# Writing a table to DRAM as one 3 MB transfer in the attention set-up, or as 16 transfers issued with the loads of the SSM stage

## Chip, cores and metric

One core of one Trainium2 chip. The metric is device microseconds of one execution. The kernel before takes 2279.62 us, the median of 3 runs (2279.33 to 2279.74).

## The reference

One layer of a hybrid decoder for a prompt of 2048 tokens and 8 sample tokens that share the weights. The input `x` is modulated, `h = x * (1 + scale) + shift`, and one product `h @ w_in` gives eight parts. `u_s` goes through a diagonal complex state-space model (SSM) of 64 groups, `q, k, v` through attention over a window of 128 keys, `z_s, z_a, g_s, g_a` are gates. Then follow a GLU product, two branch products, a gated merge, an output product and a LayerNorm.

The change concerns the relative bias of the attention, which depends on the distance of query and key alone:

```python
def rel_bias_from_dist(dist, rel_bias):
    b = rel_bias.astype(jnp.float32)[rel_bucket(jnp.clip(dist, 0, WINDOW))]
    return jnp.transpose(b, (2, 0, 1)).reshape(N_KV_HEADS, KV_GROUP, *dist.shape)
...
    s = s + rel_bias_from_dist(dist, rel_bias)
    s = jnp.where(mask[None, :, None, None], s, NEG_INF)
```

## The kernel before

**Products.** Every float32 matrix is split into a high and a low part (`split_w`, lines 49 to 60: a load into `wst`, of which there is one buffer, a cast on ACT, a subtraction on DVE), and a product is three matmuls (line 78). `products` (line 80) runs a list of jobs; a job is 128 columns of a weight against all 2056 tokens in five chunks (512, 256, 512, 264, 512 columns). A chunk is summed in one of three PSUM buffers `acc`, and an evacuation function then moves it through one of two SBUF buffers (`ev`) to DRAM. A buffer of `ev` is free again when its store has landed.

**Side work.** `products` calls `tick` three times a chunk, and each tick advances a generator of side work by one step. In phase 2 (`phase2`, line 847, 20 jobs, from 332 to about 900 us) the side work is the SSM: `ssm_pairs` (line 688) runs 32 pairs of groups through twelve steps (line 827), and a new pair starts every nine ticks. Step `load` (line 699) fetches the pair's constants `pk` (line 705) and its input `u` (line 707), each with two buffers. `b_mat` and `c_mat` are DVE work on `pk`; `t_mat` writes a small matrix `kt` to DRAM (`tD`, line 776) and reads it back skewed (`tt`, line 778); `x_in`, `scan` and `y_out` follow, and `y_out` multiplies `tt` with `u` (line 816). The first six jobs of phase 2 (`za_job`, line 540) store their chunks over SP's queue (line 550), the others over ACT's (lines 562 and 587).

**The bias table.** `attn_setup` (line 883) is the side work of the first job of phase 3. It loads a one-hot matrix `oh` and the bias `rb`, multiplies them (line 890), fills `fr`, 16 heads on 16 partitions by 384 numbers, with -1e30 (line 893), puts the scaled product in the middle (line 894), and writes each head's row 128 times to the DRAM tensor `biasD` (line 895: 3 MB, 2048 rows of 1536 bytes). Behind this it does the attention of the sample tokens (lines 897 to 976: caches `kc` and `vc`, scores, a softmax with an Exp on ACT at line 876, transposes on PE at lines 940 and 941). `attn_blocks` (line 978) then reads `biasD` with a row step of 383 (lines 1002 and 1003), so that the bias comes out shifted by one key per query.

**Order.** The order of each engine's instructions is made when the kernel is built: a list scheduler goes through the program with simulated times and gives each engine the instruction that stands first in the code of those that can go. Engines, and the queues on which SP and ACT issue transfers, then run in that order. Phase 2 pins nothing; lines 643 to 646 pin two copies to their place with `keep_in_program_order`. All transfers of SP and ACT are counted on eight semaphores in turn.

Of the kernel before, what the change touches and what calls it, by code (L numbers as in the profile page):

```python
# [9 lines left out]
F32 = mybir.dt.float32  # L10
# [29 lines left out]
class Trunk:  # L40
# [647 lines left out]
    def ssm_pairs(self, p, pp, ii):  # L688
        nc = self.nc
# [5 lines left out]
        for i in range(2):  # L695
            nc.sync.dma_start(tD[i][:, 0:112], zt)
            nc.sync.dma_start(tD[i][:, 256:368], zt)

        def load(s):
            pr = s["pr"]  # L700
            m, gl = divmod(2 * pr, 8)
            qd, gi = divmod(2 * pr, 16)
            s["m"], s["gl"] = m, gl
            s["pk"] = p.tile([128, 2, PK], F32, name="pk")
            nc.sync.dma_start(s["pk"], self.packD[qd][:, gi:gi + 2])
            s["u"] = p.tile([128, 2, 272], F32, name="u")
            nc.sync.dma_start(s["u"], self.uD[m][gl * 16:gl * 16 + 32].rearrange("c j n -> (c j) n")
                              .rearrange("(g q) n -> q g n", g=2))
# [115 lines left out]
        def gap(s):  # L824
            pass

        stages = [load, gap, b_mat, c_mat, t_mat, x_in, gap, scan, gap, gap, gap, y_out]
        return self.pipeline([{"pr": i} for i in range(32)], stages, ii)

# [50 lines left out]
        for h in range(nh):  # L880
            v.tensor_scalar(t1[:, h, kw], t1[:, h, kw], den[:, h:h + 1], None, op0=OP.mult)

    def attn_setup(self, p, pp):
        nc, I = self.nc, self.I
        oh = p.tile([32, 129], F32, name="oh")
        nc.sync.dma_start(oh, I["c_onehot"])
        rb = p.tile([32, 16], F32, name="rb")
        nc.sync.dma_start(rb, I["rel_bias"])
        pr = pp.tile([16, 129], F32, name="pt", bufs=2)
        nc.tensor.matmul(pr, rb, oh, start=True, stop=True)  # L890
        fr = p.tile([16, 384], F32, name="fr")

        nc.vector.memset(fr, NEG)
        nc.vector.tensor_scalar(fr[:, 127:256], pr, 8.0, None, op0=OP.mult)
        nc.sync.dma_start(self.biasD.rearrange("h (r l) -> h r l", l=384), fr[:, None, :].to_broadcast([16, 128, 384]))

        rr = p.tile([32, NS, 16], F32, name="rr")
        nc.vector.tensor_copy(rr, rb[:, None, :].to_broadcast([32, NS, 16]))
# [576 lines left out]
```

## Time and profile before

| | |
|---|---|
| median of 3 runs | 2279.62 us |
| profiled execution, its own time | 2282.66 us |
| its span, first to last instruction | 2280.9 us |
| mean granted TensorE clock | 0.992 |
| PE busy | 2228.4 us, 98% of the span |
| DVE, ACT, POOL busy | 1444.4, 787.7, 319.5 us |
| SP's transfer queue (q1), ACT's (q10) | 40.2%, 7.2% of 16 DMA engines |

All times in the rows are microseconds from the span's start. PE is TensorE's matmuls, DVE VectorE, ACT ScalarE, POOL GpSimd. SPq and ACTq rows are the issuing of transfers by SP and ACT. "L78" is line 78 of the kernel. `out<-in` names what an instruction writes and reads. In square brackets stands how long the engine was idle before it and what ended that.

### The profile page before, as it was taken

The page shows a single profiled execution, that of the slowest core. Times are in us where ns is not written, and L with a number is a line of the kernel's source. Part 1 is how long each engine was busy: PE and PEld are TensorE (multiplying, and loading weights), DVE is VectorE, ACT ScalarE, POOL GpSimd, SP SyncE. Part 2 cuts the span into 40 slices and gives each one's busy share as a digit, 9 for nine tenths or more (in the row PEclk, how much of TensorE's full clock was granted, in tenths as well). Part 3 has the DMA queues.
Part 4 walks back from the last instruction along what each step waited for, and adds up shares of the span by engine and source line. Part 5 has one row for each costly group of instructions (what it writes and reads, how often), then busy time and mean ns, then how long its engine had stood idle before and what let it go on. Part 6 is the DMA issues. An engine that isn't in the chain of part 4 may idle for free.

```text
span 2280.9 us, 35046 instructions
## 1 busy us (share of the span) xinstructions
PE 2228.4 (98%) x12571; PEld 1907.8 (84%) x12571; DVE 1444.4 (63%) x3572; ACT 787.7 (35%) x1700; POOL 319.5 (14%) x403
## 2 busy tenths in 40 slices
PE   7999999999999999899999999999979999999998
PEld 5888798888888888788888888888867888888886
DVE  4896219998888883168998888564454124124766
ACT  3411213332121111157777667573233123112100
POOL 1100001111111111000000000014541001222111
PEclk9999999999999999999999999999989999999999
DMA  9344523334443343743334343485347447667421
GB/s 298 103 141 143 181 96 111 115 114 119 121 117 114 114 123 110 128 126 112 114 113 138 108 119 107 113 192 180 111 143 231 124 127 241 184 186 229 158 96 72
DMA packets 387358, 317.98 MB, mean 139 GB/s; under 512 B 89318, under 2 KB 331006, under 8 KB 385599
## 3 DMA queue, kind: packets, MB, share of 16 engines
q1 hardware_dynamic: 349328, 260.02, 40.2%
q10 hardware_dynamic: 37856, 55.73, 7.2%
q8 instruction: 99, 1.62, 0.3%
q14 instruction: 75, 0.61, 0.1%
HBM read 195.24 MB, written 122.63 MB: 139 GB/s over the span
## 4 chain that ended last, share of the span: by engine, by line
PE 80%; DMA 8%; DVE 5%; SPq 3%; issue 2%; ACT 1%; POOL 1%; ACTq 0%; DVEq 0%; POOLq 0%
PE acc L78 58%; PE po L1413 8%; PE ps L1045 3%; PE po L1088 3%; PE pt L1072 2%; DMA z<-zsD 2%; PE acc L665 2%; DMA biasD<-fr 2%; SPq L178 1%; PE xp L784 1%; PE yp L817 1%; PE yp L816 1%; DMA tD<-kt 1%; DVE sg L1265 1%; DMA xst<-yD 1%
## 5 line engine op out<-in xcount | busy, mean ns | idle before, releaser
L78 PE MATMUL acc<-hh,whi 128*128 128x512 f32 (+2 forms) x2000 | 713.4, 357 | 0.1
L78 PE MATMUL acc<-hl,whi 128*128 128x512 f32 (+2 forms) x2000 | 704.7, 352 | 0.0
L78 PE MATMUL acc<-hh,wlo 128*128 128x512 f32 (+2 forms) x2000 | 702.9, 352 | 0.0
L78 PEld LDWEIGHTS acc<-hh,whi 128*128 128x128 f32 x2000 | 377.6, 189 | 49.2 <-issue 1.9
L78 PEld LDWEIGHTS acc<-hl,whi 128*128 128x128 f32 x2000 | 378.0, 189 | 48.8 <-issue 2.1
L78 PEld LDWEIGHTS acc<-hh,wlo 128*128 128x128 f32 x2000 | 377.6, 189 | 47.9 <-issue 0.8
L78 PE MATMUL acc<-xh,whi 128*128 128x512 f32 (+2 forms) x960 | 335.2, 349 | 16.3 <-ACT whi L58 16.3
L78 PE MATMUL acc<-xh,wlo 128*128 128x512 f32 (+2 forms) x960 | 333.8, 349 | 3.5 <-DVE wlo L59 3.5
L78 PE MATMUL acc<-xl,whi 128*128 128x512 f32 (+2 forms) x960 | 334.5, 349 | 0.0
L78 PEld LDWEIGHTS acc<-xh,whi 128*128 128x128 f32 x960 | 182.3, 190 | 40.8 <-ACT whi L58 17.6
L78 PEld LDWEIGHTS acc<-xh,wlo 128*128 128x128 f32 x960 | 181.9, 190 | 27.0 <-DVE wlo L59 4.1
L78 PEld LDWEIGHTS acc<-xl,whi 128*128 128x128 f32 x960 | 182.3, 190 | 22.9
L1059 ACT ACTIVATE t<-t,nm 128x256 f32<-128x256 f32 (+1 forms) x256 | 126.5, 496 | 48.0 <-DVE nm L1049 47.0
L59 DVE TENSOR_TENSOR wlo<-wst,whi 128x1024 fp32r<-128x1024 f32 x74 | 95.9, 1295 | 67.7 <-ACT whi L58 65.3
L1172 DVE TENSOR_TENSOR xl<-xst,xh 128x1024 fp32r<-128x1024 f32 (+2 forms) x84 | 97.1, 1176 | 57.9 <-ACT xh L1171 57.6
L58 ACT CAST whi<-wst 128x1024 fp32r<-128x1024 f32 x74 | 77.6, 1048 | 143.5 <-PE acc L78 121.9
L1171 ACT CAST xh<-xst 128x1024 fp32r<-128x1024 f32 (+2 forms) x84 | 86.2, 1046 | 93.3 <-PE po L1413 28.5
L1099 POOL TENSOR_TENSOR o<-o,z 128x512 f32<-128x512 f32 x32 | 43.4, 1355 | 520.5 <-DVE o L1093 474.3
L1049 DVE CUSTOM_DVE_ANT_0 t<-ps,bias,skb 128x256 f32<-128x256 f32 (+1 forms) x256 | 109.8, 471 | 5.9 <-issue 3.1
L1413 PE MATMUL po<-woh,xh 128*128 128x512 f32 (+1 forms) x272 | 103.4, 380 | 0.9 <-ACT woh L1335 0.9
L1413 PE MATMUL po<-wol,xh 128*128 128x512 f32 (+1 forms) x272 | 103.3, 380 | 0.8 <-DVE wol L1336 0.8
L1413 PE MATMUL po<-woh,xl 128*128 128x512 f32 (+1 forms) x272 | 103.3, 380 | 0.0
(359 smaller groups left out, 3318.6 us busy)
## 6 DMA issues: line engine op xcount, KB each, us to landing
wst<-in_w_in SPq DMA_DIRECT2D x50, 512.0 KB
uD<-u ACTq DMA_DIRECT2D x8, 1088.0 KB
u<-uD SPq DMA_DIRECT2D x32, 272.0 KB
yD<-y ACTq DMA_DIRECT2D x64, 132.0 KB
x<-in_x_prompt SPq DMA_DIRECT2D x16, 512.0 KB
wa<-in_w_ada SPq DMA_DIRECT2D x16, 512.0 KB
qf<-qD SPq DMA_DIRECT2D x32, 256.0 KB
z<-zaP SPq DMA_DIRECT2D x32, 256.0 KB
```

Source lines behind the costliest of these rows:

```text
L58: nc.scalar.copy(hi, st)
L59: nc.vector.tensor_tensor(lo, st, hi, op=OP.subtract)
L78: self.nc.tensor.matmul(ps[:, :n], w[:, k, :], x[:, k, :], start=(k == 0 and i == 0), stop=(k == KT - 1 and i == 2))
L665: nc.tensor.matmul(ps[:mt, :256], x[:, k, ts], w[:, k, :], start=(i == 0), stop=(i == 23))
L1045: nc.tensor.matmul(ps[:, a2, kw], s["q"][e][:, 2 * g + a2], kk[:, g, kw], start=(i == 0), stop=(i == 1))
L1049: v.tensor_tensor_reduce(t1[:, h, kw], ps[:, a2, kw], s["bias"][:, 4 * g + h, b0:b0 + kw.stop], -0.125, nsk[:, hs:hs + 1], OP.add, OP.min, ...
L1059: nc.scalar.activation(t1[:, h, kw], t1[:, h, kw], AF.Exp, bias=nm[:, h:h + 1], scale=-1.0, accum_out=den[:, h:h + 1])
L1072: nc.tensor.transpose(pt[:, a], s["t", g][:, a, h * 128:(h + 1) * 128], self.ident)
L1088: nc.tensor.matmul(pr, s["v"][h][:, g], x.rearrange("p a q -> p (a q)"), start=(h == hs[0] and i == 0), stop=(h == hs[-1] and i == 1))
L1171: nc.scalar.copy(xv(hi[:, k - 1:k + 1]), sv(st))
L1172: nc.vector.tensor_tensor(xv(lo[:, k - 1:k + 1]), sv(st), xv(hi[:, k - 1:k + 1]), op=OP.subtract)
L1413: nc.tensor.matmul(ps[:, :w], X[a][:, k, ts], Wo[h * w // 512][b][:, k, ws], start=(i == 0), stop=(i == 23))
```

## The change

The table is made at the start of phase 2, from `ssm_pairs`, and written there: step `load` of pairs 16 to 31 issues one transfer each, of one head's row 128 times (192 KB), ahead of the pair's own loads. `attn_setup` keeps its loads of `oh` and `rb`, which it needs for the sample tokens, and loses the rest.

```diff
@@ ssm_pairs
             nc.sync.dma_start(tD[i][:, 0:112], zt)
             nc.sync.dma_start(tD[i][:, 256:368], zt)
 
+        fr = self.bias_rows(p, pp)
+
         def load(s):
             pr = s["pr"]
+            if pr >= 16:
+
+                h = pr - 16
+                nc.sync.dma_start(self.biasD[h:h + 1].rearrange("h (r l) -> h r l", l=384),
+                                  fr[h:h + 1, None, :].to_broadcast([1, 128, 384]))
             m, gl = divmod(2 * pr, 8)
@@ attn_setup
+    def bias_in(self, p):
+        oh = p.tile([32, 129], F32, name="oh", bufs=1)
+        self.nc.sync.dma_start(oh, self.I["c_onehot"])
+        rb = p.tile([32, 16], F32, name="rb", bufs=1)
+        self.nc.sync.dma_start(rb, self.I["rel_bias"])
+        return oh, rb
+
+    def bias_rows(self, p, pp):
+
+        nc = self.nc
+        oh, rb = self.bias_in(p)
+        pr = pp.tile([16, 129], F32, name="tr", bufs=1)
+        nc.tensor.matmul(pr, rb, oh, start=True, stop=True)
+        fr = p.tile([16, 384], F32, name="fr", bufs=1)
+
+        nc.vector.memset(fr, NEG)
+        nc.vector.tensor_scalar(fr[:, 127:256], pr, 8.0, None, op0=OP.mult)
+        return fr
+
     def attn_setup(self, p, pp):
         nc, I = self.nc, self.I
-        oh = p.tile([32, 129], F32, name="oh")
-        nc.sync.dma_start(oh, I["c_onehot"])
-        rb = p.tile([32, 16], F32, name="rb")
-        nc.sync.dma_start(rb, I["rel_bias"])
-        pr = pp.tile([16, 129], F32, name="pt", bufs=2)
-        nc.tensor.matmul(pr, rb, oh, start=True, stop=True)
-        fr = p.tile([16, 384], F32, name="fr")
-
-        nc.vector.memset(fr, NEG)
-        nc.vector.tensor_scalar(fr[:, 127:256], pr, 8.0, None, op0=OP.mult)
-        nc.sync.dma_start(self.biasD.rearrange("h (r l) -> h r l", l=384), fr[:, None, :].to_broadcast([16, 128, 384]))
+        oh, rb = self.bias_in(p)
```

## Rows read from the trace of the kernel before

**Rows 1.** The page, part 1: busy time of each engine

```profile
PE 2228.4 (98%) x12571; PEld 1907.8 (84%) x12571; DVE 1444.4 (63%) x3572; ACT 787.7 (35%) x1700; POOL 319.5 (14%) x403
```

**Rows 2.** Waits of PE, whole span: us in total, times, longest

```profile
PE pt L940 <- DVE t1s L881: 5.8, 1, 5.8
```

**Rows 3.** Timeline of PE, 936 to 966: start, us, engine, what, count

```profile
943.34 0.39 PE L78 MATMUL acc<-hl,whi 128*128 128x512 f32 x1
949.51 0.45 PE L940 MATMUL pt<-ident,t1s 128*128 128x128 f32 x1 [5.79 <-DVE t1s L881]
...
950.39 0.63 PE L78 MATMUL acc<-hh,whi 128*128 128x512 f32 x1
...
954.97 0.40 PE L78 MATMUL acc<-hh,wlo 128*128 128x512 f32 x1
```

**Rows 4.** Stretch 950 to 960: us, busy of PE, PEld, DVE, ACT, POOL, granted clock, DMA share, GB/s

```profile
950.00:960.00 10.00, 10.00 (x57) 6.48 (x57) 2.14 (x4) 1.53 (x2) 0.00 (x0) 0.76 0.32 96
```

**Rows 5.** Timeline of ACT, 900 to 985

```profile
928.86 0.58 ACT L586 COPY zr<-acc 128x512 f32<-128x512 f32 x1 [10.67 <-DMA zsD<-zr]
...
946.76 1.28 ACT L876 ACT_TABLE_LOAD   x1 [0.47 <-DMA biasD<-fr]
948.06 0.40 ACT L876 ACTIVATE t1s<-t1s,nm 128x129 f32<-128x129 f32 x1
```

**Rows 6.** Timeline of DVE, 900 to 985

```profile
937.51 0.15 DVE L873 TENSOR_TENSOR es<-sk,mxs 128x1 f32<-128x1 f32 x1
```

**Rows 7.** Chain that ended last, 860 to 1060: start, us, what

```profile
909.93 36.83 DMA biasD<-fr
```

**Rows 8.** Timeline of SP's issues, 840 to 1010

```profile
904.01 0.55 SPq L886 DMA_DIRECT2D oh<-in_c_onehot  x1
...
909.93 0.68 SPq L895 DMA_DIRECT2D biasD<-fr  x1
918.99 33.92 SPq L55 DMA_DIRECT2D wst<-in_w_in  x2
```

**Rows 9.** SP's own waits, 900 to 1010: us in total, times, longest

```profile
SPq L55 <- DMA wst<-in_w_in: 28.5, 1, 28.5
...
SPq L1003 <- DMA zsD<-zr: 4.0, 2, 3.1
```

**Rows 10.** Line 1215, in the code of phase 4: durations, first and last start

```profile
L1215 SPq DMA_DIRECT2D bglu<-in_b_glu x1: 1268/1268/1268, 40.7 to 40.7; - x1
```

**Rows 11.** Timeline of SP's issues, 330 to 400

```profile
332.50 0.85 SPq L705 DMA_DIRECT2D pk<-packD  x1
...
336.12 0.47 SPq L705 DMA_DIRECT2D pk<-packD  x1
336.63 0.44 SPq L707 DMA_DIRECT2D u<-uD  x1
341.06 3.70 SPq L550 DMA_DIRECT2D zaP<-z  x2
...
349.04 0.38 SPq L778 DMA_DIRECT2D tt<-tD  x1
```

**Rows 12.** Timeline of PE, 351 to 354

```profile
352.51 0.61 PE L816 MATMUL yp<-u,tt 128*128 128x264 f32 x2
```

**Rows 13.** Transfer queues, 920 to 930: packets, MB, share of 16 engines

```profile
q1 hardware_dynamic: 615, 0.94, 87.8%
```

**Rows 14.** Transfer queues, 728 to 730, one store of 256 KB

```profile
q10 hardware_dynamic: 144, 0.26, 34.9%
```

**Rows 15.** Transfer queues, 330 to 332, one store of 128 KB

```profile
q10 hardware_dynamic: 144, 0.13, 19.4%
```

**Rows 16.** Stretch 700 to 750: us, busy by engine, clock, DMA share, GB/s

```profile
700.00:750.00 50.00, 50.00 (x275) 42.22 (x274) 42.46 (x90) 9.51 (x21) 10.54 (x14) 1.00 0.42 124
```

**Rows 17.** Timeline of SP's issues, 700 to 760

```profile
723.44 0.34 SPq L705 DMA_DIRECT2D pk<-packD  x1
```

**Rows 18.** Timeline of DVE, 703 to 745

```profile
725.93 0.49 DVE L716 TENSOR_TENSOR tmp<-pk 128x128 f32<-128x128 f32 x2
```

## The prediction

> **What bounds the kernel.** I read the page first: PE is busy for 98% of the span [rows 1], so whatever leaves PE idle is paid in full, and work on other engines costs only what makes PE wait. Next come PE's own waits. Of the places where it waits inside the phases that the change touches, one stands out: 5.8 us at line 940, for the softmax of the sample tokens [rows 2]. The timelines around it show why. PE had finished its last possible matmul at 943.34 and went on at 949.51 [rows 3]. Behind that wait the granted clock of 950 to 960 is 0.76 [rows 4]: for about half of the stretch PE ran at 1.2 GHz and not at 2.4, and matmuls of 512 columns took 0.63 us where they take 0.40 [rows 3]. DVE had everything ready for the Exp at 937.7 [rows 6], but ACT came to it only at 946.76 [rows 5], because ACT works in order and its copies ahead of it waited for an `ev` buffer, 10.67 us in the row shown, whose store had not landed [rows 5]. The stores were late because of the bias table. Its write lies on the chain for 36.83 us from 909.93 on [rows 7], and in 920 to 930 SP's queue holds 87.8% of the 16 DMA engines for 0.94 MB [rows 13]. SP's ring suffers as well: the weights asked for at 918.99 [rows 8] kept SP waiting for 28.5 us [rows 9].
>
> So the reader is to see two things: a stall of some 8 us that this write causes, and a write that is very slow for its 3 MB.
>
> **What the change removes.** If the write is gone from 909.93, ACT's stores land in time. The Exp then starts at 937.7 plus its table load of 1.28 us [rows 5, 6], and PE's transposes follow 949.51 - 948.06 = 1.45 us behind the Exp [rows 3, 5]: at 940.4, ahead of 943.34, so nothing is waited for. What is gained is 5.8 us, and the clock's share, 10 us x 0.24 = 2.4 us [rows 2, 4]: **-8.2 us**. Next behind it is nothing that PE waits for. The matmul of line 890, the memset and the scaling move to the start of phase 2 beside full engines, at 0.3 to 0.4 us each; I cost them at nothing either way. The loads of `oh` and `rb` are now made twice; two issues of half a microsecond on SP [rows 8] come ahead of the first `pk` load, and the cover is PE's matmuls of that stage, or one microsecond if it is gone.
>
> **What one new transfer costs.** No row has a transfer like it: 192 KB, read 128 times from one row of one partition. I bound it. Below: the old write, with 16 source partitions, moved 0.94 MB in 10 us [rows 13], so 196,608 bytes take 2.1 us if only the bytes count. Above: if each source partition gives no more than its share of that rate, one partition takes 16 times as long, 33 us. That the engines were not the limit is in the rows: 615 packets at 87.8% of 16 engines are 228 ns for 1536 bytes [rows 13], whereas a store from 128 partitions, each packet a row of its own partition, costs 11.17 engine-us for 128 packets of 2048 bytes [rows 14], 87 ns each. The source side set the pace. The nearest rows to one partition read by one engine at a time are the two stores: twice the bytes cost 11.17 - 6.21 = 4.96 engine-us more [rows 14, 15], that is 39 ns for 1024 bytes, 26 bytes per ns. At that pace 196,608 bytes take **7.4 us**, and I take this: a row of a partition given out at the best rate that any row shows for one, however many engines ask. Sixteen of them hold SP's rings for 119 us, where the single write needed 37.
>
> The Trainium skill, page "SBUF — State Buffer", section "Door 1: The DMA port swizzle", speaks against this change: transfers are limited by how many of 16 ports their partitions reach, it has 104 GB/s for partitions 0 to 15 and 27.6 GB/s for 0 to 3. This trace agrees on the first (94 GB/s in rows 13) and has nothing for the second; an estimate by that page is 7.1 us per transfer and 114 us for all, 5 us less in the sum below.
>
> **Where they stand in SP's order.** The code puts them in step `load` of pairs 16 to 31. But the trace shows that a transfer's place in the code doesn't hold it back: a load of phase 4 is issued at 40.7 [rows 10], and the loads of pair 1, nine ticks behind those of pair 0 in the code, went out at 336.12 and 336.63 right behind them and ahead of the first chunk's store at 341.06 [rows 11]. What held back later loads was a buffer that wasn't free. The new transfers need `fr` and nothing else. From the load of `oh` to the old write 5.9 us passed [rows 8]; with SP free for phase 2 at 332.5 [rows 11] the first transfer goes out at 338.4. SP issues one every 0.51 us (336.12 to 336.63), and in the 10.6 us up to the `tt` load of pair 0 at 349.04 [rows 11] 13 to 16 of them fit beside four of its own. So I expect all of them in a burst at the start of the stage, not in its second half.
>
> **What waits behind them.** SP's queue carries in this stage the stores of the first six jobs, `pk`, `u`, `tD`, `tt` and the weights. `tt` of pair 0 reaches PE 3.5 us after its issue (349.04 to 352.51) [rows 11, 12]; PE can't pass that matmul. With all 16 ahead, the rings are free at 338.4 + 119 = 457, PE goes on at 461 and has lost 108 us. With 13 ahead it goes on 22 us earlier and loses 86, and the last three then hold `z` stores for 22 us, of which PE covers some 14 with the chunks for which it has buffers (the same 14 that lie between 338.4 and 352.5): 94. I take 100. Stores on ACT's queue share the engines and wait too, as in [rows 5], but in these jobs they are few. A wait of this kind brings one slow stretch of the clock, 2.4 us [rows 4]. DVE's later work shifts with PE; its idle time, 7.5 us in 50 [rows 16], takes up the rest.
>
> **Sum.** The profiled execution takes 2282.66 us, 3 us above the median of the runs, of which 2280.9 are span; all terms are from it and I put them on the median: 2279.6 - 8.2 + 100 + 2.4 = **2374 us**. Its own range, with 86 to 115 us for the loss, is 2358 to 2390. Differences under 0.2% (4.6 us) can't be told from no change.
>
> **Rivals.**
> - *As written.* The transfers keep their places, one per pair in pairs 16 to 31, ahead of that pair's `pk` load. For it: the code. Against it: [rows 10, 11]. A `pk` load is used by DVE as soon as it is there (723.44 to 725.93, 2.5 us) [rows 17, 18], so 7.4 us in the ring ahead of it make DVE wait; it has 7.5 of 50 us idle [rows 16], 2.5 in the 17 us of a pair, and 4.9 x 16 = 78 us go to PE. 2279.6 - 8.2 + 78 = 2350.
> - *Cheap transfers in a burst.* Only the bytes count, 2.1 us each, 34 in all. The rings are free at 372, PE goes on at 376, 23 us late: 2279.6 - 8.2 + 23 + 2.4 = 2297. For it: the engines' sum is what [rows 13] shows. Against it: they all ask one partition.
> - *Hidden transfers, faster than before.* The transfers cost 2.1 us and stand one per pair; DVE's 2.5 idle us of each pair take them, and only the removed stall counts: 2271.4. It decides where a transfer takes less than 2.5 us and the code's places hold. Against it is what speaks against both of the above.
> - *The write doesn't cause the stall.* If other transfers make ACT late at 918 to 946, the 8.2 us stay: forecast 2382, hidden transfers 2279.6. [rows 13] leaves little room for others.
>
> **Chances.** Forecast 0.58, as written 0.12, cheap burst 0.12, faster 0.12, no change 0.03, much slower (towards 33 us per transfer) 0.03. The range leaves out the faster cases, no change and the far end: 2290 to 2400. Faster by over 0.2%: 0.12; within 0.2%: 0.03; slower: 0.85.
>
> **What would show it.** Right: sixteen issues of `biasD` at SP between 338 and 360; PE's waits led by line 816 or 817 for `tt`, or by `acc` for a `z` store, with about 100 us in all; the page's PE row low in the slices from 350 to 460; the row of line 940 gone and the clock of 950 to 960 (shifted) at 1.00. A wait of DVE at line 716 for `pk`, 16 times, would mean the code's places held. The forecast is wrong if SP issues the transfers elsewhere, or if in their stretch SP's queue moves much more than 27 GB/s.

## The result and the profile after

The changed kernel takes **2371.39 us** (median of 5 runs, 2370.73 to 2375.24) where the kernel before, run beside it, takes 2279.74 (2279.33 to 2281.26): ratio 1.041, interval 1.0397 to 1.0424. It is 91.7 us slower. Its profiled execution took 2371.21 us, of which 2369.3 are span.

The page of the changed kernel: span, busy time of each engine, then PE's busy share, its clock and the DMA share in 40 slices of 59.2 us, and SP's queue.

```profile
span 2369.3 us, 35075 instructions
...
PE 2231.8 (94%) x12571; PEld 1910.6 (81%) x12571; DVE 1441.6 (61%) x3572; ACT 788.3 (33%) x1700; POOL 321.3 (14%) x403
...
PE   7999991399999999999999999999979999999998
...
PEclk9999995699999999999999999999989999999999
DMA  9353638733343343333433533368337546667521
...
q1 hardware_dynamic: 349664, 260.04, 41.4%
```

The work is the same as in [rows 1]: as many matmuls, as much busy time within 4 us. But in two slices, 355 to 474 us, PE stands nearly still while the DMA engines are at their fullest since the first slice. PE's idle time, span less busy, rose from 52.5 us [rows 1] to 137.5, by 85.0; its busy time rose by 3.4. Together that is the whole difference of the spans, 88.4 us.

PE's waits in the changed kernel, whole span (us in total, times, longest):

```profile
PE yp L823 <- DMA tt<-tD: 62.6, 2, 60.5
PE tr L752 <- DVE bt L725: 22.5, 1, 22.5
...
PE tr L752 <- DVE kt L779: 9.1, 1, 9.1
```

The wait at the softmax [rows 2] is gone, and these three came, 94.2 us together. Line 823 is line 816 of the kernel before, the matmul that needs `tt`; `bt` is what DVE makes of `pk`. Their places on PE's timeline (the idle time before each in brackets):

```profile
366.17 0.66 PE L752 MATMUL tr<-ident,bt 128*128 128x128 f32 x2 [9.09 <-DVE kt L779]
...
432.31 1.25 PE L823 MATMUL yp<-u,tt 128*128 128x264 f32 x2 [60.51 <-DMA tt<-tD]
...
465.10 0.66 PE L752 MATMUL tr<-ident,bt 128*128 128x128 f32 x2 [22.50 <-DVE bt L725]
```

In [rows 12] PE passed the matmul of `tt` at 352.51; here it does so at 432.31. Why `tt` came so late stands on the timeline of SP's issues (start, time that SP spent on them, line, what, count):

```profile
336.40 0.47 SPq L712 DMA_DIRECT2D pk<-packD  x1
336.91 0.43 SPq L714 DMA_DIRECT2D u<-uD  x1
340.61 0.32 SPq L550 DMA_DIRECT2D zaP<-z  x1
343.83 1.21 SPq L706 DMA_DIRECT2D biasD<-fr  x2
345.14 4.30 SPq L550 DMA_DIRECT2D zaP<-z  x1
349.84 18.13 SPq L706 DMA_DIRECT2D biasD<-fr  x3
368.07 5.62 SPq L550 DMA_DIRECT2D zaP<-z  x1
373.74 15.11 SPq L706 DMA_DIRECT2D biasD<-fr  x3
388.95 7.24 SPq L550 DMA_DIRECT2D zaP<-z  x1
396.23 5.17 SPq L706 DMA_DIRECT2D biasD<-fr  x2
401.50 11.88 SPq L783 DMA_DIRECT2D tD<-kt  x2
413.43 2.71 SPq L706 DMA_DIRECT2D biasD<-fr  x2
420.14 3.35 SPq L785 DMA_DIRECT2D tt<-tD  x1
423.53 19.64 SPq L706 DMA_DIRECT2D biasD<-fr  x4
443.27 7.25 SPq L712 DMA_DIRECT2D pk<-packD  x1
```

All 16 transfers of the table go out at the start of the stage, between 343.83 and 443, not in its second half. Twelve of them stand ahead of `tt`, which is issued at 420.14 and not at 349.04 [rows 11], and four behind it, ahead of `pk` of the third pair; that `pk` is the 22.5 us at line 752. The third wait, 9.1 us at 366.17, is a `z` store: ACT could not write its next `z` before a store behind the first two transfers of the table, issued at 345.14, had landed, and DVE's `z` and `kt` stood behind ACT (waits in 350 to 370):

```profile
ACT z L546 <- DMA zaP<-z: 16.7, 1, 16.7
DVE z L547 <- ACT z L546: 15.8, 1, 15.8
```

The second column of SP's timeline was not foreseen: 18.13 us for three issues. Over all 16 (shortest, median and longest in ns, first and last start):

```profile
L706 SPq DMA_DIRECT2D biasD<-fr x16: 568/3975/7305, 343.8 to 435.9; - x16
```

SP could not pass its transfers on any faster than the queue took them.

The queues in 345 to 445, the GB/s in 40 slices of 2.5 us, and packets, MB and share of 16 engines:

```profile
GB/s 30 28 26 28 26 66 42 27 29 26 26 66 43 76 53 27 28 28 25 28 28 28 81 27 26 27 28 30 63 28 27 27 28 27 81 28 24 28 28 28
...
q1 hardware_dynamic: 2986, 3.53, 84.9%
```

Wherever only the table moves, the rate is 24 to 30 GB/s, with the engines 84.9% busy. The packets of the table, the only ones of 1536 bytes, begin at 345.05, and the last of them starts at 460.62: 115.6 us for all 16, 7.2 us each.

Stretches of the changed kernel (us, busy of PE, PEld, DVE, ACT, POOL, granted clock, DMA share, GB/s):

```profile
376.00:400.00 24.00, 0.00 (x0) 0.00 (x0) 0.00 (x0) 0.86 (x2) 0.00 (x0) 0.51 0.85 36
400.00:420.00 20.00, 0.00 (x0) 0.00 (x0) 0.00 (x0) 0.00 (x0) 0.00 (x0) 0.50 0.81 39
...
1040.00:1060.00 20.00, 20.00 (x126) 15.53 (x125) 2.77 (x7) 3.83 (x12) 0.00 (x0) 1.00 0.33 89
```

From 376 to 420 all engines stand still but for two instructions of ACT (0.86 us). The transpose that ended the old stall, line 940 of the kernel before, now starts at 1042.9; in 1040 to 1060, which answers to [rows 4], PE is busy throughout at a clock of 1.00: the old stall is really gone.

### The profile page after: what moved, and what is told of

It reads as the page before. It is cut to its first block, busy times and chain, and to the rows that moved or that the text cites. A ratio compares the mean times of both kernels' runs of the same rounds, so it can differ in the third digit from the quotient of the medians.

```text
span 2369.3 us, 35075 instructions
## 1 busy us (share of the span) xinstructions
PE 2231.8 (94%) x12571; PEld 1910.6 (81%) x12571; DVE 1441.6 (61%) x3572; ACT 788.3 (33%) x1700; POOL 321.3 (14%) x403
## 4 chain that ended last, share of the span: by engine, by line
PE 82%; DMA 6%; SPq 4%; DVE 4%; issue 2%; POOL 1%; ACT 1%; DVEq 0%; ACTq 0%; POOLq 0%
PE acc L78 60%; PE po L1429 7%; PE ps L1061 3%; PE po L1104 2%; DMA z<-zsD 2%; PE pt L1088 2%; PE acc L665 2%; SPq L706 2%; PE xp L791 1%; SPq L178 1%; PE yp L823 1%; PE yp L824 1%; DMA pk<-packD 1%; DMA tD<-kt 1%; DMA zaP<-z 1%
## 5 line engine op out<-in xcount | busy, mean ns | idle before, releaser
L1188 DVE TENSOR_TENSOR xl<-xst,xh 128x1024 fp32r<-128x1024 f32 (+2 forms) x84 | 97.7, 1181 | 52.5 <-ACT xh L1187 51.9
```

Source lines behind the costliest of these rows:

```text
L1188: nc.vector.tensor_tensor(xv(lo[:, k - 1:k + 1]), sv(st), xv(hi[:, k - 1:k + 1]), op=OP.subtract)
```

## The experiments

The theory: a transfer's price is set by the source partitions that it reads, the 16 go out in a burst because nothing holds them to their place, and what PE lost is `tt`, `z` stores and `pk` behind them. The rivals: the bytes or the number of issues cost it; the place does, whatever is put there; the code's place held. The medians of the kernel before beside these runs were 2279.08, 2279.24 and 2278.11.

**Same bytes, same issues, same place, other source partitions.** The row of each head is made on 8 partitions; transfer h writes one 1536-byte row from each of the 128.

```diff
-        nc.tensor.matmul(pr, rb, oh, start=True, stop=True)
-        fr = p.tile([16, 384], F32, name="fr", bufs=1)
+        nc.vector.tensor_copy(r8, rb[:, :, None].to_broadcast([32, 16, 8]))
+        nc.tensor.matmul(pr, r8.rearrange("b h s -> b (h s)"), oh, start=True, stop=True)
+        fr = p.tile([128, 384], F32, name="fr", bufs=1)
...
-                nc.sync.dma_start(self.biasD[h:h + 1].rearrange("h (r l) -> h r l", l=384),
-                                  fr[h:h + 1, None, :].to_broadcast([1, 128, 384]))
+                nc.sync.dma_start(self.biasD.rearrange("h (s r l) -> (h s) r l", s=8, l=384)[:, h:h + 1],
+                                  fr[:, None, :].to_broadcast([128, 1, 384]))
```

> Edit: the changed kernel with the same 16 transfers of the same 196,608 bytes at the same place in the code, but fr is held on 128 partitions (8 copies of each head's row) and each transfer reads one row from every partition. Number of issues, bytes and place stay; only the source partitions of a transfer differ. Theory (a transfer is paced by its single source partition, 7.2 us; the lost time is tt behind about 115 us of such transfers): each transfer takes 0.6 to 1.5 us (192 KB at the rate of a store from 128 partitions, 11.17 engine-us for 128 packets of 2048 bytes, is 1.05 us), all 16 done within 25 us, PE's waits at tt fall from 62.6 to under 15 us, time 2275 to 2290 us. Rival 1 (the bytes or the number of issues cost it, whatever the source): 2360 to 2375 us. Rival 2 (DRAM rows are the limit, not the source): transfers stay at about 7 us, 2360 to 2375 us.

Measured: 2275.42 us, ratio 0.9986 (0.9977 to 0.9995). The burst is still there, 16 issues from 344.6 to 355.1, all ahead of `tt`, which follows at 357.54. Its busy times, its issues of the table, and its queue in 346 to 356:

```profile
PE 2224.9 (98%) x12571; PEld 1906.0 (84%) x12571; DVE 1442.7 (63%) x3573; ACT 788.2 (35%) x1700; POOL 325.3 (14%) x403
```

```profile
L706 SPq DMA_DIRECT2D biasD<-fr x16: 320/450/617, 344.6 to 355.1; - x16
```

```profile
q1 hardware_dynamic: 2604, 3.24, 93.3%
```

3.24 MB pass in 10 us where the changed kernel needed 100 for 3.53. An issue takes SP 0.45 us in the median, against 3.98 in the changed kernel. So neither the bytes, nor the 16 issues, nor the place of the burst cost much: 96 of the 2371 us hang on the source partitions. (The 1.05 us of the expectation are twice what its own rows give, 0.52 over 16 engines; measured are 0.6.) One thing more changes with this edit: the rows of one transfer land 24 KB apart in DRAM and not in one run of 192 KB, and no run changes that alone. The run with the heads in another order, below, speaks for the source: there each transfer still writes its run of 192 KB. In spans, 2369.3 less 2273.2, that is 89.2 us of PE's idle time and 6.9 of busy time at a slower clock.

**The move alone: one transfer of 16 heads at the start of the stage.**

```diff
         fr = self.bias_rows(p, pp)
+        nc.sync.dma_start(self.biasD.rearrange("h (r l) -> h r l", l=384), fr[:, None, :].to_broadcast([16, 128, 384]))
...
-            if pr >= 16:
...
```

> Edit: the changed kernel, but one transfer of all 16 heads (16 source partitions, the form that the kernel before had in its later stage) right behind the rows of fr, at the start of the SSM stage. Theory (rate goes with the source partitions): this transfer takes 33 to 38 us in place of 115, tt of pair 0 lands some 80 us earlier than in the changed kernel, PE's waits there are 15 to 35 us in place of 94, time 2287 to 2310 us. Rival (the place is what costs, whatever the transfer's length): 2350 to 2375.

Measured: 2298.21 us, ratio 1.0081 (1.0066 to 1.0096). `tt` is issued at 382.33. PE waits 18.3 us for `z`, whose stores stood behind the table, and 3.5 for `tt`. The queue in 350 to 380:

```profile
q1 hardware_dynamic: 2100, 3.09, 88.5%
```

That is 103 GB/s from 16 partitions. The move costs 19 us net, not 92.

**The split alone: 16 transfers in the old place.**

```diff
-        nc.sync.dma_start(self.biasD.rearrange("h (r l) -> h r l", l=384), fr[:, None, :].to_broadcast([16, 128, 384]))
+        for h in range(16):
+            nc.sync.dma_start(self.biasD[h:h + 1].rearrange("h (r l) -> h r l", l=384),
+                              fr[h:h + 1, None, :].to_broadcast([1, 128, 384]))
```

> Edit: the kernel before with its one transfer split by head into 16, in its old place behind the SSM stage; nothing is moved. This is the other half of the change alone (e_one_early is the move without the split: 2298.21 us). Theory (split by head, each transfer reads one partition and takes 7.2 us wherever it stands): 115 us in place of 37 for the whole write, from 910 to about 1026, the wait at the softmax of the sample tokens grows from 5.8 us and new waits for stores and for the reads of the table come behind it; 78 us longer for the rings, of which PE covers a part, so 2310 to 2365 us. Rival (the price of 7.2 us belongs to the place at the start of the stage, where other transfers compete): the 16 take 40 to 60 us in all, 2275 to 2295.

Measured: 2345.22 us, ratio 1.0299 (1.0282 to 1.0316). The packets run from 914.5 to 1019.3, 105 us, and SP is held for nearly all of that at its issues; PE waits in the stage behind:

```profile
911.21 97.29 SPq L896 DMA_DIRECT2D biasD<-fr  x16
```

```profile
PE acc L78 <- ACT zr L586: 49.1, 2, 41.6
PE pt L942 <- DVE t1s L881: 11.6, 1, 11.6
PE po L964 <- DVE so L959: 3.0, 1, 3.0
```

The price does not belong to the place. The split costs 67 us where the old write stood, and there the old stall grows from 5.8 to 11.6 us.

**The places held.** Each transfer is pinned to its place in the program's order.

```diff
-                nc.sync.dma_start(self.biasD[h:h + 1].rearrange("h (r l) -> h r l", l=384),
-                                  fr[h:h + 1, None, :].to_broadcast([1, 128, 384]))
+                self.tc.keep_in_program_order(
+                    nc.sync.dma_start(self.biasD[h:h + 1].rearrange("h (r l) -> h r l", l=384),
+                                      fr[h:h + 1, None, :].to_broadcast([1, 128, 384])))
```

> Edit: the changed kernel with each of the 16 transfers pinned to its place in the order of the program, so that they go out one by one over the second half of the SSM stage, as the code says. Price of a transfer as before, 7.2 us from one partition. Theory (burst ahead of tt is where the time went, and the price is per transfer): PE's waits at 366 to 465 us are gone, no transfer of the table before 600 us; each transfer still takes about 7.2 us of SP's rings and a load asked for behind it lands so much later. What that costs was put at 78 us (4.9 us in each of 16 pairs, 2350 us) if pk is used as soon as it is there; if SP's rings have room for it, between 0 and 30 us (2272 to 2305). Rival (the transfers cost the same wherever they stand, since each holds SP's rings): 2360 to 2375.

Measured: 2337.55 us, ratio 1.0254 (1.024 to 1.0268). The 16 issues are spread over the second half, the first at 563.7 (none was expected before 600) and the last at 900.9, and PE's stall at 366 to 465 is gone. Its busy times, the issues, PE's waits in 550 to 940, and that stretch (its granted clock is the third number from the end):

```profile
PE 2245.2 (96%) x12571; PEld 1918.8 (82%) x12571; DVE 1442.1 (62%) x3572; ACT 788.5 (34%) x1700; POOL 321.5 (14%) x403
```

```profile
L707 SPq DMA_DIRECT2D biasD<-fr x16: 492/510/4789, 563.7 to 900.9; - x16
```

```profile
PE yp L824 <- DMA tt<-tD: 24.8, 6, 5.3
PE yp L825 <- DVE S L816: 16.1, 5, 8.2
```

```profile
550.00:940.00 390.00, 349.14 (x1770) 289.41 (x1769) 274.28 (x574) 63.39 (x129) 50.30 (x106) 0.94 0.54 107
```

So the burst accounts for about 34 us of the loss, and a spread-out write at this price still costs 64 against the next experiment: 4.0 us in each of 16 pairs. The expectation left a gap between 30 and 78 us, and the result fell into it, nearer to its upper end. Two thirds of it are waits; the rest is a slower clock, 0.94 in this stretch where the next experiment has 1.00. Against the next experiment, which differs in the source alone, PE is idle for 40.6 us more (87.1 against 46.5) and busy for 21.0 us more (2245.2 against 2224.2).

**The places held and the cheap source**: the pin and the 128 source partitions together.

```diff
+                self.tc.keep_in_program_order(
+                    nc.sync.dma_start(self.biasD.rearrange("h (s r l) -> (h s) r l", s=8, l=384)[:, h:h + 1],
+                                      fr[:, None, :].to_broadcast([128, 1, 384])))
```

> Edit: the transfers pinned to their places in the second half of the SSM stage as in e_pin, and each read from 128 partitions as in e_16_128. This is the change as its code says, with a cheap transfer. Theory (price and burst are two separate causes; at about 1 us a transfer is hidden beside pairs that have 2.5 us to spare): the wait at the softmax is gone and nothing takes its place, 2269 to 2273 us, as in e_128_old (2270.24). Rival (16 more issues in SP's queue among the loads of the pairs cost by themselves): 2275 to 2285.

Measured: 2273.09 us, ratio 0.9975 (0.9965 to 0.9984). At 0.6 us a transfer (3.24 MB in 10 us, above) it is hidden, and only the old stall goes. The time is at the upper end of what was expected, 2.9 us above the last experiment below; the intervals of the two don't tell them apart.

**Four transfers of four neighbouring heads.**

```diff
-            if pr >= 16:
+            if pr >= 16 and pr % 4 == 0:
...
-                nc.sync.dma_start(self.biasD[h:h + 1].rearrange("h (r l) -> h r l", l=384),
-                                  fr[h:h + 1, None, :].to_broadcast([1, 128, 384]))
+                nc.sync.dma_start(self.biasD[h:h + 4].rearrange("h (r l) -> h r l", l=384),
+                                  fr[h:h + 4, None, :].to_broadcast([4, 128, 384]))
```

> Edit: the changed kernel with four transfers of four heads each (4 neighbouring source partitions, 786,432 bytes) in place of 16 of one head; the bytes, the place and the burst stay. Two readings of the slow source are told apart. Reading A (a group of four neighbouring partitions shares one way out of about 27 GB/s): each transfer takes 28 to 30 us, 112 to 118 us in all, time 2360 to 2376, as in the changed kernel. Reading B (each partition gives about 27 GB/s by itself): each takes 7 to 8 us, about 30 us in all, time 2280 to 2300.

Measured: 2388.18 us, ratio 1.048 (1.0466 to 1.0494). The queue in 350 to 406 (56 us):

```profile
q1 hardware_dynamic: 1008, 1.47, 22.6%
```

Again some 25 GB/s, with the packets of all four running from 346.0 to 468.3, 122 us: as reading A has it. The share matters here: 22.6% is between three and four of 16 engines' worth of time. Four partitions by some four engines give what one partition gave to some fourteen (84.9%), so neither the engines' time nor the single partition set the rate; it fits a limit that the four neighbours share. By itself this run leaves a rival: with only some four engines at work, each packet takes 0.20 us (22.6% of 16 engines, 1008 packets in 56 us), and if that were what an engine needs for a packet of a repeated row, the rate would be the same. Two runs speak against it: in the last experiment below each row is repeated 16 times and a packet takes 0.065 us (101.1% of 16 engines for 1742 packets in 7 us), and the next run changes the order of the heads alone. The Trainium skill, page "SBUF — State Buffer", section "Door 1: The DMA port swizzle", gives 27.6 GB/s for partitions 0 to 3 and 104 for 0 to 15; the runs agree with 25 and 103. The time came out 12 us above what was expected: here one `z` store stands at SP behind the second transfer and another behind the fourth, and PE waits 54.5 and 50.7 us behind ACT, which waits for them.

**The heads in another order**: 0, 4, 8, 12, 1, 5, ...

```diff
-                h = pr - 16
+                h = pr % 4 * 4 + pr // 4 % 4
```

> Edit: the changed kernel with the heads in the order 0, 4, 8, 12, 1, 5, ... so that neighbouring transfers read from different groups of four partitions; everything else stays. In the changed kernel the one transfer that followed another of a different group took 5.5 us and the others 7.0 to 7.5. Theory (groups of four are the limit, and a ring works its transfers off in order, so two transfers overlap only at their ends): 5 to 6 us each, 80 to 100 us in all, PE's waits there 60 to 78 us, time 2338 to 2358. Rival A (several transfers in flight at once, each on its own group): about 30 to 45 us in all, 2285 to 2305. Rival B (no overlap): 2365 to 2375.

Measured: 2339.97 us, ratio 1.0267 (1.0252 to 1.0283). The packets run from 345.6 to 429.7, 84 us, 5.3 each. The order of the transfers alone is worth 31 us. The queue in 362 to 366, in which only the table moves:

```profile
q1 hardware_dynamic: 166, 0.22, 81.5%
```

That is 55 GB/s, twice the rate of the changed kernel, at about the same share of the engines. So transfers from two groups of four pass side by side, where neighbours of one group do not, and this is what shows the group. They do so for a part of the time only: four side by side throughout would take about 29 us in all, not 84. That they overlap just at their ends, because the queue works them off in turn, is the theory's reading.

**Another queue**: the transfers issued by POOL.

```diff
-                nc.sync.dma_start(self.biasD[h:h + 1].rearrange("h (r l) -> h r l", l=384),
+                nc.gpsimd.dma_start(self.biasD[h:h + 1].rearrange("h (r l) -> h r l", l=384),
```

> Edit: the changed kernel with the 16 transfers issued from POOL's queue and not from SP's; source, bytes and place in the code stay. Theory (what PE lost was tt, z stores and loads behind the transfers in SP's own queue, and SP held up at issuing them): the transfers still take 7 us each or more, 115 us or more in all, but tt of pair 0 is landed within 10 us of its issue and PE's waits at 366 to 465 are under 40 us, time 2285 to 2325. Rival (the 16 DMA engines themselves are held, so the queue makes no difference): PE's waits there 80 us or more, 2355 to 2380.

Measured: 2354.18 us, ratio 1.033 (1.0316 to 1.0344). This is against the theory's number and near the rival's, 0.8 us under its range: PE waits 81.3 us in one piece for `tt`. Its queues in 350 to 400, and SP's issues:

```profile
q0 software_dynamic: 502, 1.54, 91.3%
q1 hardware_dynamic: 374, 0.46, 3.8%
```

```profile
340.75 17.73 SPq L550 DMA_DIRECT2D zaP<-z  x4
358.60 23.47 SPq L783 DMA_DIRECT2D tD<-kt  x2
440.06 0.38 SPq L785 DMA_DIRECT2D tt<-tD  x1
```

POOL's queue (q0) holds 91.3% of the engines for 31 GB/s, and SP's gets 0.46 MB through in 50 us. `tt` itself passes quickly now, but the `tD` stores that it reads, asked for from 358.60 on, land only at 426 and 440. So in this run the slow transfers held up SP's queue from another one, and the move to it saved 17 of the 92 us.

**The old place and form, but the source on 128 partitions** (one transfer of all heads in the kernel before).

```diff
-        nc.sync.dma_start(self.biasD.rearrange("h (r l) -> h r l", l=384), fr[:, None, :].to_broadcast([16, 128, 384]))
+        nc.sync.dma_start(self.biasD.rearrange("h (s r l) -> (h s) r l", s=8, l=384),
+                          fr[:, None, :].to_broadcast([128, 16, 384]))
```

> Edit: the kernel before with its one transfer in its old place, but fr on 128 partitions (8 copies of each head's row), so that the write reads 128 partitions and not 16. Theory (the write is slow by its source partitions, and its 37 us make ACT's stores late and PE wait at the softmax of the sample tokens): the write takes 8 to 12 us, that wait of 5.8 us and the slow clock behind it are gone, time 2271 to 2274 us, 0.2 to 0.4% under the kernel before. Rival (the stall has another cause): 2278 to 2281.

Measured: 2270.24 us, ratio 0.9964 (0.9952 to 0.9977), the lowest median of all and a little under the expected 2271. The write's packets run from 914.1 to 923.2, 9.1 us. The queues in 915 to 922, and two stretches:

```profile
q1 hardware_dynamic: 1742, 2.68, 101.1%
```

```profile
940.00:950.00 10.00, 10.00 (x54) 7.59 (x56) 1.70 (x3) 1.53 (x2) 0.00 (x0) 1.00 0.31 94
950.00:960.00 10.00, 10.00 (x75) 7.92 (x68) 1.07 (x4) 2.30 (x10) 0.00 (x0) 1.00 0.32 84
```

2.68 MB in 7 us is 383 GB/s where the old write had 94 [rows 13]. PE waits for nothing from 900 to 1000, and the clock of 950 to 960 is 1.00, not 0.76 [rows 4]. What the change wanted, the stall away, is had without moving anything: 8.8 us by the medians.

## Why the prediction was right

It gave 2374 us and 2290 to 2400; the time is 2371.39. Step by step:

- *The stall that is removed, -8.2.* Right. The kernel with the fast write in its old place gained 8.8 us, with an interval from 5.2 to 10.9, and lost both the wait and the slow stretch behind it.
- *One transfer, 7.4 us between 2.1 and 33.* Right: 7.2. The pace of 26 bytes per ns that was read from two stores [rows 14, 15] stands in the profile after as 24 to 30 GB/s. But the reason given, a row of one partition given out at its best rate, was too narrow: four partitions together give no more. That the pace fitted is in part luck, since those two stores don't tell the pace of an engine from that of its source. The text's sum for all 16 was 119 us; measured were 115.6. The estimate by the Trainium skill, page "SBUF — State Buffer", section "Door 1: The DMA port swizzle", 7.1 us and 114 in all, came nearer.
- *Not held to their place.* Right: all 16 went out at the start, and pinning them moved them to the second half. Begun at 343.8 and not at 338.4, because `fr` was ready 5.4 us later than put.
- *13 to 16 of them ahead of `tt`.* A near miss, and by luck. It was 12, but the way of counting failed: SP began at 343.8, and at 0.51 us per issue only ten would have fitted in up to 349.04. The time that SP has at run time doesn't set the order; the order is made when the kernel is built. The changed kernel and the one with the heads in another order issue in the same sequence, 12 ahead of `tt`, though SP was held there for different times; with the source on 128 partitions all 16 stand ahead. Nor did the working have the held issues, 3.98 us in the median and up to 7.3.
- *100 us lost.* 94.2 us by the three waits. PE passed the matmul of `tt` 79.8 us later than in [rows 12], where 86 were put for 13 transfers ahead; 69.6 of these were idle (9.1 for the `z` store and 60.5), and the rest PE filled with other work. What came behind cost more than put: 22.5 us for `pk` of the third pair, where the step had 8 for `z` stores and did not name `pk`. The two errors offset each other.
- *The clock, +2.4.* PE's busy time rose by 3.4 us although the old slow stretch went (2.4), so the new ones cost about 5.8: it was mis-sized, since there are three waits and not one.
- *The sum.* By the profiled executions 2371.21 - 2282.66 = 88.6, by the medians 91.7; the prediction's terms add up to 94.2. Its own range, 2358 to 2390, is a little wider than what 86 and 115 us give, 2360 to 2389.

Of the rivals, *as written* was priced at 78 us for 16 places held; the pinned kernel shows 64. The wait for `pk` which that rival named is there, 27.6 us in 5 waits of DVE, but DVE waits longer for `tD` (35.8 us in 9), and what PE waits for is `tt` and the scan behind it. *Cheap transfers in a burst* is the kernel with 128 source partitions: 2275.42 against 2297 put, because a transfer costs about 0.6 us there, not 2.1. *Hidden transfers* is the pinned kernel with that source: 2273.09 against 2271.4 put.

Move and split each alone cost 19.1 and 67.1 us, together 86.2; the change, with both, 91.7. What is left between these is small beside the terms, and no run was made for it.

## What to carry to other kernels

Before a transfer is split, count the partitions that each piece reads: here one piece per head took three times as long as one piece for all, and a source copied over 128 partitions took about a twelfth of it. Look up where a moved transfer is really issued, since its place in the code bound nothing here; and ask what is queued behind it. If a stall comes from a slow transfer, try first to make the transfer fast where it is.

## What the runs showed that was not expected

- SP is held at its issues behind slow transfers: 97.29 us for 16 issues in the old place, where an issue with the fast source took 0.45 us. Whatever SP has to issue next waits: the next two loads of weights in the old place went out from 1008.60 on, where the kernel before issued them from 918.99 on.
- Another queue was hardly a way around it: with 91.3% of the engines' time in POOL's queue at 31 GB/s, SP's first `tD` store, 64 KB, landed 67 us after SP came to it.
- Many short waits cost PE more clock than one long one. Against the same kernels with the cheap source, the pinned one had 40.6 us more idle time and 21.0 us more busy time, the burst 89.2 and 6.9. In the long wait, PE idle, the granted clock fell to 0.50 (1.2 GHz), but there was nothing to slow down. What costs is the work behind a wait: behind the one that ended at 366.17 in the changed kernel, matmuls of 512 columns took 0.63 us until 369.2, and 0.40 from 369.6 on.
